# Softmax attention walked by token tile, with one norm chain for ten heads, and three operand sets prepared earlier, in an encoder block on one core

## The chip, the cores and the metric

The kernel runs on one core of one Trainium2 chip. The metric is the device time in microseconds (us) of one execution. Five engines work in parallel, each through its own list of instructions in order: PE (TensorE, matmuls; PEld is its weight load), DVE (VectorE), ACT (ScalarE), POOL (GpSimd, nearly unused here) and SP (SyncE, which issues all transfers between HBM and the on-chip memory).

## The reference

One layer over 1024 tokens of width 1024, all in float32. From `h = RMSNorm(x)` one projection gives the inputs of two branches. Cut to what matters here:

```python
h = _rms_norm(x, norm_mix_g[l]);  proj = h @ w_in[l]
# branch A: bidirectional gated linear attention, 4 heads, per-head RMSNorm, times silu(r)
y_gla = _gla_branch(g_q, g_k, g_v, g_r, g_lr_f, g_lr_b, ...) @ w_o_gla[l]
# branch B: softmax attention, 8 query heads on 2 key heads, head size 128, window +-128
q = _rope(_rms_norm(q, q_g), pos);  k = _rope(_rms_norm(k, k_g), pos)
p = exp(scores - m);  o = p / (p.sum() + exp(sink - m)) @ v
merged = sigmoid(gate_a) * y_gla + sigmoid(gate_b) * y_swa
x = x + merged @ w_out[l]
x = x + (silu(ff_gate) * ff_up) @ w_ffn_out[l]      # after a second RMSNorm
```

## The kernel before, in words

**Products.** Every float32 operand is split into a high part (an ACT copy to the float32r type) and a low part (a DVE subtraction), and every product is three matmuls: high x high, high x low, low x high (`mm3`, L77 to L80, and `product`, L811 to L817). A 512-column matmul is the unit of the work; 24 of them (8 pieces of the 1024 inner elements, three matmuls each) make one 128x512 result.

**The dense list.** Up to L912 the program interleaves two kinds of work on PE. One is `dense`, a list of generators (L552) whose steps are single 512-column matmuls: projections with tokens on the columns (`proj_f`, 48 steps each), projections with tokens on the rows (`proj_t`, 192 steps: 96 for the first half `s=0` of the tokens, 96 for the second) and `first_halves` (192 steps, the first half of the gate projections). In all 1824 steps. `fill(n)` issues n steps. The weights of a projection arrive 128x512 at a time by `next_unit`, two ahead. For `proj_t` the first pass splits each weight tile and stores both parts to HBM (`wkeep`, one load and two stores of 256 KB per 12 steps); the second pass loads both parts again (`wagain`, two loads, no splitting).

**Slots.** The other kind is the chain of small stages of the two attention branches, written into numbered slots. `slot(stages, n)` issues the slot's stages and spreads n dense steps between them, so that PE has matmuls to do while ACT and DVE prepare the next stage. The tables `GF` and `SF` give n. The order on PE is exactly the order of the program; on the other engines a scheduler sets the order from its own estimate when the kernel is built, and it can move an instruction far ahead of its place in the program.

**Gated linear attention** (slots with `GF`, 4 heads x 8 chunks). It opens with `fill(24)`, and its first PE stage, the gate matmuls of `g_gates` (`z`), needs `lrS`, the low-rank codes, which DVE writes last in `lr_out` (L313) after the norm statistics (`rsqrt`, L93 to L102). In slots 0 to 7 `x_sums` also forms differences of quarters of the normalised x (the sets T1, T2, 22, T3, T4) and stores them to HBM. They feed a seven-product scheme for the second half of the gate projections.

**Softmax attention** (slots with `SF`). There are 16 items: group g (4 heads) and token tile t. Before the change item n is `g, t = divmod(n, 8)`: all tiles of group 0, then all of group 1. An item goes through six consecutive slots: `a_prep` (load, squares, sums, norm factor, rotation), `a_turn` (transposes on PE), `a_scores`, `a_probs` (transposes of the probabilities), `a_out`. Keys are prepared by `k_prep` and `k_turn` for one tile per slot during the first 8 slots. The last four slots only drain the pipeline, with 15 dense steps each.

**The second half of the gates** (L900 to L912). `xpart` loads a set from HBM, ACT and DVE split it. The sets T1, T2 and 22 (12 tiles) are split here, each followed by 4 dense steps, then the remaining dense steps run, then `second_first(0)` forms a sum of weights `s1` (DVE, L808), splits it and multiplies it with T1 into bank Z; `second_rest(f)` follows for f = 0 to 7 with products by T2 (bank X), 22 (Z), T3 (X) and T4 (X). After each `second_rest(f)`, `prep_a(0, f)` prepares one of the eight tiles (`oa`) that the next stage, `branch_a(0)`, multiplies with w_oa: two loads, a sigmoid on ACT (L895), two DVE products, and the split (L825, L826).

**Staging.** `stage()` takes one of four 128x512 buffers for results that go out to HBM and for some loads.

## Time and profile before

| What | Value |
|---|---|
| Median of 3 runs (lowest, highest) | 1684.49 us (1682.74, 1684.93) |
| The profiled execution: its time, its span | 1679.58 us, 1677.3 us |
| PE busy, matmuls | 1655.2 us (99%), 7788 |
| DVE busy, ACT busy | 1237.9 us (74%), 857.1 us (51%) |
| Mean granted TensorE clock | 0.996 |
| Moved by the DMA engines | 300.13 MB, mean 179 GB/s |

The span runs from the first to the last instruction of the profiled execution. The clock is the share of full speed that TensorE was granted. Rows of the timeline begin with the start time and the duration in us; a bracket at the end of a row gives the idle time of that engine just before the instruction and what ended it. Matmuls overlap, so a row's duration is longer than the distance from start to start; the distance is what counts.

### The profile page before, as it was taken

How to read it: one execution, taken by the hardware profiler on the slowest of the kernel's cores; microseconds unless marked ns; L12 is line 12 of the kernel's file. 1: busy time of each engine (PE TensorE's matmuls, PEld its weight loads, DVE VectorE, ACT ScalarE, POOL GpSimd, SP SyncE). 2: the span in 40 equal slices, each digit the busy share in tenths (PEclk: the TensorE clock that was granted, in tenths of full speed). 3: DMA queues.
4: the chain of work that ended last, by engine and by line, in shares of the span. 5: the costliest groups of instructions: out<-in, count | busy, mean ns of one | idle time of the engine just before them, and what ended most of it. 6: DMA issues, size and time to landing. Idle time of an engine off the chain costs nothing.

```text
span 1677.3 us, 23798 instructions
## 1 busy us (share of the span) xinstructions
PE 1655.2 (99%) x7788; PEld 1372.9 (82%) x7788; DVE 1237.9 (74%) x2570; ACT 857.1 (51%) x1809; POOL 0.2 (0%) x4
## 2 busy tenths in 40 slices
PE   9999999999999998999999999999999999999999
PEld 6788888887888876887888888788888888888887
DVE  8786777853997767876673568887778877789755
ACT  7454677865687674334553556533333333344443
POOL 0000000000000000000000000000000000000000
PEclk9999999999999999999999999999999999999999
DMA  8875656668533238656764545344224543595433
GB/s 286 297 259 186 200 185 227 226 196 284 185 108 107 82 113 285 227 193 214 217 213 143 190 134 180 113 136 134 91 92 144 164 157 131 177 323 192 143 102 119
DMA packets 183547, 300.13 MB, mean 179 GB/s; under 512 B 20894, under 2 KB 46238, under 8 KB 183424
## 3 DMA queue, kind: packets, MB, share of 16 engines
q1 hardware_dynamic: 183424, 298.62, 54.4%
q8 instruction: 61, 1.00, 0.3%
q14 instruction: 62, 0.51, 0.1%
HBM read 203.12 MB, written 95.42 MB: 178 GB/s over the span
## 4 chain that ended last, share of the span: by engine, by line
PE 91%; DVE 3%; DMA 3%; ACT 2%; issue 1%; SPq 0%; ACTq 0%; DVEq 0%
PE mm L75 35%; PE ch L75 8%; PE mm L815 7%; PE mm L816 7%; PE mm L817 7%; PE mm L1177 7%; PE ch L1177 5%; PE ch L815 3%; PE ch L817 3%; PE ch L816 3%; PE mm L244 2%; PE ch L747 1%; DMA xr<-xT 1%; PE ch L546 0%; PE ch L697 0%
## 5 line engine op out<-in xcount | busy, mean ns | idle before, releaser
L69 ACT ACTIVATE wh<-wr 128x512 fp32r<-128x512 f32 x198 | 123.8, 628 | 115.1 <-PE mm L75 84.5
L71 DVE TENSOR_TENSOR wl<-wr,wh 128x512 fp32r<-128x512 f32 x198 | 135.7, 686 | 32.0 <-ACT wh L69 29.1
L794 ACT ACTIVATE wh<-ws 128x512 fp32r<-128x512 f32 x120 | 75.5, 631 | 148.7 <-PE mm L816 84.6
L75 PE MATMUL mm<-wl,xh 128*128 128x512 f32 x320 | 127.0, 397 | 1.2 <-DMA wl<-wl 1.2
L75 PE MATMUL mm<-wh,xh 128*128 128x512 f32 x320 | 127.7, 399 | 0.4 <-DVE st L136 0.4
L75 PE MATMUL mm<-wh,xl 128*128 128x512 f32 x320 | 127.9, 400 | 0.0
L75 PE MATMUL mm<-xh,wh 128*128 128x512 f32 x256 | 102.5, 401 | 0.3 <-ACT wh L69 0.3
L75 PE MATMUL mm<-xl,wh 128*128 128x512 f32 x256 | 102.0, 398 | 0.3 <-DVE xl L323 0.3
L794 ACT ACTIVATE wh<-wr 128x512 fp32r<-128x512 f32 x60 | 37.9, 632 | 105.4 <-issue 49.6
L795 DVE TENSOR_TENSOR wl<-ws,wh 128x512 fp32r<-128x512 f32 x120 | 82.1, 685 | 12.8 <-ACT wh L794 12.8
L75 PE MATMUL mm<-xh,wl 128*128 128x512 f32 x256 | 88.6, 399 | 0.0
L794 ACT ACTIVATE wh<-a 128x512 fp32r<-128x512 f32 x66 | 41.7, 632 | 90.6 <-PE mm L1177 42.4
L795 DVE TENSOR_TENSOR wl<-a,wh 128x512 fp32r<-128x512 f32 x66 | 45.5, 690 | 39.2 <-ACT wh L794 38.1
L75 PEld LDWEIGHTS mm<-wl,xh 128*128 128x128 f32 x320 | 60.5, 189 | 12.6 <-DMA wl<-wl 1.6
L75 PEld LDWEIGHTS mm<-wh,xh 128*128 128x128 f32 x320 | 60.7, 190 | 10.5 <-DVE st L136 0.8
L1177 PE MATMUL mm<-hh,wh 128*128 128x512 f32 x176 | 68.6, 390 | 0.5 <-DVE c L1115 0.5
L75 PEld LDWEIGHTS mm<-wh,xl 128*128 128x128 f32 x320 | 60.7, 190 | 10.2
L1177 PE MATMUL mm<-hl,wh 128*128 128x512 f32 x176 | 68.5, 389 | 0.0
L1177 PE MATMUL mm<-hh,wl 128*128 128x512 f32 x176 | 68.5, 389 | 0.0
L1150 DVE TENSOR_TENSOR hl<-hr,hh 128x512 fp32r<-128x512 f32 x77 | 52.7, 686 | 6.8 <-ACT hh L1149 6.7
L75 PEld LDWEIGHTS mm<-xl,wh 128*128 128x128 f32 x256 | 48.2, 188 | 7.6 <-DVE xl L323 0.6
L75 PEld LDWEIGHTS mm<-xh,wh 128*128 128x128 f32 x256 | 48.2, 188 | 7.4 <-ACT wh L69 0.5
(546 smaller groups left out, 4875.0 us busy)
## 6 DMA issues: line engine op xcount, KB each, us to landing
wr<-in_w_fi_dram SPq DMA_DIRECT2D x102, 256.0 KB, 2.8
wr<-in_w_f_dram SPq DMA_DIRECT2D x80, 256.0 KB, 3.4
wh<-wh SPq DMA_DIRECT2D x80, 256.0 KB, 2.9
wl<-wl SPq DMA_DIRECT2D x80, 256.0 KB, 3.0
B<-c SPq DMA_DIRECT2D x44, 256.0 KB, 2.1
T<-st SPq DMA_DIRECT2D x44, 256.0 KB, 2.6
a<-in_w_fo_dram SPq DMA_DIRECT2D x44, 256.0 KB, 5.3
hr<-T SPq DMA_DIRECT2D x44, 256.0 KB, 2.7
```

The costliest lines, as they stand in the source:

```text
L69: nc.scalar.activation(h, raw, AF.Copy)
L71: nc.vector.tensor_tensor(l, raw, h.bitcast(F32), op=ALU.subtract)
L75: nc.tensor.matmul(o, a, b, start=start, stop=stop)
L244: nc.tensor.matmul(Y[q], w[:, c], x, start=f0, stop=f1, skip_group_check=True)
L747: nc.tensor.transpose(pt[:, h], a.p[:, h, (kb - a.b0) * P:(kb - a.b0 + 1) * P], ident)
L794: nc.scalar.activation(h, src, AF.Copy)
L795: nc.vector.tensor_tensor(l, src, h.bitcast(F32), op=ALU.subtract)
L815: nc.tensor.matmul(o, h[:, c], x[kk][0], start=start and kk == 0, stop=False, skip_group_check=True)
L816: nc.tensor.matmul(o, h[:, c], x[kk][1], start=False, stop=False, skip_group_check=True)
L817: nc.tensor.matmul(o, l[:, c], x[kk][0], start=False, stop=kk == nk - 1, skip_group_check=True)
L1150: nc.vector.tensor_tensor(l, r, h.bitcast(F32), op=ALU.subtract)
L1177: nc.tensor.matmul(ys[m], a[:, c], b, start=f0, stop=f1, skip_group_check=True)
```

## The change

1. `rsqrt`: the correction step takes two DVE instructions ahead of the last one instead of three, and its first one now reads the result of the ACT exponential.
2. `proj_t` takes the half `s` as an argument. The second-half passes of `skv`, `sq0` and `sq1` move behind all three first-half passes; before, each was followed by its own second half.
3. The opening fill of the gated linear attention grows from 24 to 36 dense steps, and `x_sums` comes one slot later, behind the slot's stages.
4. Softmax attention goes by token tile: item n is `t, g = divmod(n, 2)`. One `prep(t)` per tile loads both groups of tile t and the keys and values of tile t+1, and computes one chain of squares, sums and norm factors for the ten heads; `a_rope` keeps the rotation. The output copy takes a buffer of `stage()` instead of one of its own.
5. The buffers `xn` live for the whole program, and `xpart` uses them. T1 and 22 are loaded and split in the four drain slots of the softmax attention (one tile of each per slot); only T2 stays behind them, with 8 dense steps after each tile.
6. `prep_a(0, f)` comes ahead of `second_rest(f)`, and `prep_a(0, 7)` ahead of `second_rest(6)`.

The number of matmuls and the number of issued transfers are the same.

```diff
@@ rsqrt
-            nc.vector.tensor_scalar(t, v, scale, epsv, op0=ALU.mult, op1=ALU.add)
-            nc.vector.tensor_tensor(t, t, l, op=ALU.mult)
-            nc.vector.scalar_tensor_tensor(t, t, -0.5, l, op0=ALU.mult, op1=ALU.mult)
+            nc.vector.scalar_tensor_tensor(t, l, -0.5 * scale, l, op0=ALU.mult, op1=ALU.mult)
+            nc.vector.scalar_tensor_tensor(t, v, epsv / scale, t, op0=ALU.add, op1=ALU.mult)
             nc.vector.scalar_tensor_tensor(dst, t, 1.5, l, op0=ALU.add, op1=ALU.mult)
...
         stg = root.enter_context(tc.tile_pool(name="stg", bufs=4))
+        xn = root.enter_context(tc.tile_pool(name="xn", bufs=4))
...
-        def proj_t(name, n):
-            for f in (wkeep, wagain):
-                plan.extend((lambda f=f, k=k: f(n, k)) for k in range(KT))
+        def proj_t(name, n, s):
+            plan.extend((lambda k=k: (wkeep, wagain)[s](n, k)) for k in range(KT))
...
-        dense += [proj_t("v0", 0), proj_f("q1", 2), proj_f("k1", 3), proj_f("q2", 4), proj_f("k2", 5),
-                  proj_t("v1", 1), proj_f("q3", 6), proj_f("k3", 7), proj_t("skv", 2), proj_t("sq0", 3),
-                  proj_t("sq1", 4)] + [proj_f(f"r{m}", 8 + m) for m in range(8)] + [first_halves()]
-
-        xn = glas.enter_context(tc.tile_pool(name="xn", bufs=4))
+        dense += [proj_t("v0", 0, 0), proj_t("v0", 0, 1), proj_f("q1", 2), proj_f("k1", 3), proj_f("q2", 4), proj_f("k2", 5),
+                  proj_t("v1", 1, 0), proj_t("v1", 1, 1), proj_f("q3", 6), proj_f("k3", 7), *(proj_t(nme, n, s) for s in range(2)
+                                                          for nme, n in (("skv", 2), ("sq0", 3), ("sq1", 4)))] + [proj_f(f"r{m}", 8 + m) for m in range(8)] + [first_halves()]
...
-            fill(24)
+            fill(36)
             for t in range(last + 1):
-                if t < 8:
-                    x_sums(t)
                 slot([(lambda v=at[t, j]: v[0](*v[1:])) if (t, j) in at else None for j in (0, 5, 4, 3, 2, 1)], share(GF, t))
+                if 1 <= t <= 8:
+                    x_sums(t - 1)
...
+        def prep(t):
+            sq = sw.tile([P, 10, P], F32, tag="sq", name=nm("sq"), bufs=1)
+            lo, hi = 8, 8
+            if t >= 0:
...
+                for g in range(2):
+                    need((f"sq{g}", t))
+                    nc.sync.dma_start(out=qr[:, 4 * g:4 * g + 4].rearrange("p a b -> p (a b)"), in_=scr[f"sq{g}", t])
+                nc.scalar.activation(sq[:, 0:8], qr, AF.Square)
+            if t + 1 < KT:
...
+                nc.scalar.activation(sq[:, 8:10], kv[:, 0:2], AF.Square)
+            ss = sw.tile([P, 10], F32, tag="ss", name=nm("ss"))
+            nc.vector.tensor_reduce(ss[:, lo:hi], sq[:, lo:hi], axis=mybir.AxisListType.X, op=ALU.add)
+            rs = sw.tile([P, 10], F32, tag="rs", name=nm("rs"), bufs=4)
+            rsqrt(rs[:, lo:hi], ss[:, lo:hi], 1.0, EPS * 128, eps128, sw, (P, hi - lo), f"sn{hi - lo}")
+            if t + 1 < KT:
+                keys[t + 1] = rope_k(kv, rs[:, 8:10], t + 1)
...
-            ob = sw.tile([P, 4, P], F32, tag="ob", name=nm("sob"))
+            ob = stage((P, 4, P))
...
         def xpart(q, k):
-            r = tp.tile([P, HT], F32, tag="xr", name=nm("xr"), bufs=8)
+            r = xn.tile([P, HT], F32, tag="xn", name=nm("xn"))
...
         for n in range(2 * KT):
-            g, t = divmod(n, KT)
+            t, g = divmod(n, 2)
...
-            todo[n + 1].append((a_prep, g, t))
-            if n < KT:
-                todo[n + 1].append((k_turn, n))
-                todo[n].append((k_prep, n))
-        order = (k_prep, a_prep, a_scores, a_turn, k_turn, a_out, a_probs)
+            todo[n + 1].append((a_rope, g, t))
+            if g == 0:
+                todo[n + 1].append((prep, t))
+                if t + 1 < KT:
+                    todo[n + 2].append((k_turn, t + 1))
+        order = (prep, a_rope, a_scores, a_turn, k_turn, a_out, a_probs)
...
                 slot([lambda e=e: e[0](*e[1:]) for e in v], share(SF, t))
+                if t >= 2 * KT + 2:
+                    assert len(dense) == 1
+                    for q in ("T1", "22"):
+                        xpart(q, t - 2 * KT - 2)
...
-            for q in ("T1", "T2", "22"):
-                for k in range(4):
-                    xpart(q, k)
-                    fill(4)
+            homes["T2"] = tp, "t2h{}", "t2l{}", 0
+            for k in range(4):
+                xpart("T2", k)
+                fill(8)
             fill(1 << 30)
...
             for f in range(len(PAIRS)):
+                if f < 7:
+                    prep_a(0, f)
+                if f == 6:
+                    prep_a(0, 7)
                 second_rest(f)
-                prep_a(0, f)
```

The order of instructions shows the change at three places. **First, DVE where the dense list ends.** `L808`/`L835` are the sums of weights (`ws`) for `second_first(0)` and `second_rest(0)`, `L795`/`L822` their low parts, `L247`/`L245` the results (`st`) of `first_halves`, of which PE's last dense matmul releases the last one; `L826`/`L774` are low parts of the operand sets. Before:

```order
L826 TENSOR_TENSOR xl_2126_8829<-xr_8826,xh_2125_8828 128x512
L808 TENSOR_TENSOR ws_8875<-wr_8871,wr_2132_8873 128x512
L808 TENSOR_TENSOR ws_8949<-ws_8875,wr_8869 128x512
L247 TENSOR_TENSOR st_8865<-mm_8756,rstd 128x512
L795 TENSOR_TENSOR wl_8879<-ws_8875,wh_8878 128x512
```

and, nine rows further on:

```order
L826 TENSOR_TENSOR xl_2157_8933<-xr_8930,xh_2156_8932 128x512
L826 TENSOR_TENSOR xl_2160_8939<-xr_8936,xh_2159_8938 128x512
L864 TENSOR_TENSOR nt_8946<-ch_8877,nt_8942 128x512
L869 TENSOR_TENSOR nt_8967<-mm_8948,nt_8942 128x512
L808 TENSOR_TENSOR ws_8969<-wr_2162_8944,ws_8949 128x512
```

Now:

```order
L245 TENSOR_TENSOR st_8512<-mm_8402,rstd 128x512
L71 TENSOR_TENSOR wl_8613<-wr_8609,wh_8611 128x512
L835 TENSOR_TENSOR ws_8675<-wr_8671,wr_2073_8673 128x512
L835 TENSOR_TENSOR ws_8761<-ws_8675,wr_8669 128x512
L245 TENSOR_TENSOR st_8575<-mm_8403,rstd 128x512
L822 TENSOR_TENSOR wl_8679<-ws_8675,wh_8678 128x512
L245 TENSOR_TENSOR st_8605<-mm_8579,rstd 128x512
L822 TENSOR_TENSOR wl_8764<-ws_8761,wh_8763 128x512
L774 TENSOR_TENSOR xl_2080_8697<-xn_8694,xh_2079_8696 128x512
L835 TENSOR_TENSOR ws_8781<-wr_2108_8756,ws_8761 128x512
L774 TENSOR_TENSOR xl_2083_8703<-xn_8700,xh_2082_8702 128x512
L245 TENSOR_TENSOR st_8633<-mm_8580,rstd 128x512
```

Before, the first sum `s1` (`ws_8875`) came just ahead of the last result of `first_halves`, behind the parts of 22, and the sum `s4` (`ws_8969`) came behind bank reads `nt` that wait for products. Now `s1`, `s2` and `s4` all stand ahead of the third result from the end (`st_8633`).

**Second, ACT around the last `oa` tile.** `sg` is the sigmoid of `prep_a`, `oah` the high part of its tile, `wh` of L69 the weights of `branch_a(0)`, `wh` of L794/L821 those of the second half of the gates. Before:

```order
L69 ACTIVATE wh_10040<-wr_10038 128x512
L69 ACTIVATE wh_10063<-wr_10061 128x512
L69 ACTIVATE wh_10081<-wr_10079 128x512
L895 ACTIVATE sg_9933<-st_9931 128x512
L825 ACTIVATE oah_2400_9937<-st_9929 128x512
```

Now:

```order
L903 ACTIVATE sg_9526<-st_9524 128x512
L821 ACTIVATE wh_9701<-ws_9699 128x512
L773 ACTIVATE oah_2296_9530<-st_9522 128x512
L821 ACTIVATE wh_9721<-wr_2316_9609 128x512
L69 ACTIVATE wh_9781<-wr_9779 128x512
```

The last `oah` stood behind the sixth weight tile of `branch_a(0)`; now it stands ahead of the first.

**Third, SP where the softmax attention begins.** `cosb` to `sink` are its constants, `kvr` the first keys and values, `sq_*` stores of a `proj_t` pass that is ending, `wh`/`wl` the kept weights of the pass that follows (the number after the name is the weight tile k). Before:

```order
L62 DMA cosb<-in_c_cos_dram 128x512
L62 DMA sinb<-in_c_sin_dram 128x512
L62 DMA band<-in_c_band_dram 128x384
L62 DMA qg<-in_qg_dram 128x128
L62 DMA kg<-in_kg_dram 128x128
L62 DMA sink<-in_sink_dram 128x8
L663 DMA kvr_5663<-skv_3683 128x512
L220 DMA sq_0_5704<-st_5705 128x512
L220 DMA sq_1_5714<-st_5715 128x512
L220 DMA sq_2_5724<-st_5725 128x512
L220 DMA sq_3_5734<-st_5735 128x512
L168 DMA wl_5744<-wl_2_5377 128x512
```

Now:

```order
L167 DMA wl_5741<-wl_3_4409 128x512
L62 DMA cosb<-in_c_cos_dram 128x512
L62 DMA sinb<-in_c_sin_dram 128x512
L62 DMA band<-in_c_band_dram 128x384
L62 DMA qg<-in_qg_dram 128x128
L62 DMA kg<-in_kg_dram 128x128
L62 DMA sink<-in_sink_dram 128x8
L661 DMA kvr_5669<-skv_3618 128x512
L218 DMA sq_6_5705<-st_5706 128x512
L218 DMA sq_7_5715<-st_5716 128x512
L167 DMA wh_5739<-wh_3_4407 128x512
```

Behind the constants the first weight part still to come was that of tile k=2, after four stores; now it is that of k=3, after two.

More of the change, by code (lines that the diff above doesn't have):

```diff
@@ L189, in proj_f @@
             return steps()
[L191 to L193 removed]
+        def proj_t(name, n, s):
+            plan.extend((lambda k=k: (wkeep, wagain)[s](n, k)) for k in range(KT))
             def steps():
[L196 removed]
+                if True:
                     b = [mmtile() for _ in range(4)]
@@ L625, in body, with rope_k @@
         nc.vector.tensor_tensor(qB[:, :, 64:128], sinb, gb_[0], op=ALU.mult)
[L627 to L645 removed]
+        nc.vector.tensor_scalar(kg, kg, 128 ** 0.5, None, op0=ALU.mult)
+        for h in range(8):
+            for s in range(2):
+                scr["b", h, s] = scratch(f"b{h}_{s}")
+        keys, att = {}, {}
+        def rope_k(raw, rs, t):
+            qn = sw.tile([P, 2, P], F32, tag="qn2", name=nm("qn"))
+            b = sw.tile([P, 2, P], F32, tag="sq2", name=nm("sq"))
+            for h in range(2):
+                nc.vector.scalar_tensor_tensor(qn[:, h], raw[:, h], rs[:, h:h + 1], kg, op0=ALU.mult, op1=ALU.mult)
+            c = cosb[:, t:t + 1].to_broadcast([P, 2, 64])
+            s = sinb[:, t:t + 1].to_broadcast([P, 2, 64])
             nc.vector.tensor_tensor(b[:, :, 0:64], qn[:, :, 64:128], s, op=ALU.mult)
@@ L764, in a_out, with xsplit, xpart @@
                                   in_=ob[:, h])
+        XT = {q: [] for q in ("T1", "T2", "22", "T3", "T4")}
+        def xsplit(pool, th, tl, src):
+            h = pool.tile([P, HT], FR, tag=th, name=nm(th))
+            l = pool.tile([P, HT], FR, tag=tl, name=nm(tl))
+            nc.scalar.activation(h, src, AF.Copy)
+            nc.vector.tensor_tensor(l, src, h.bitcast(F32), op=ALU.subtract)
+            return h, l
+        homes = {"T1": (xp, "xh{}1", "xl{}1", 0), "22": (xp, "xh{}1", "xl{}1", 4),
+                 "T3": (xp, "xh{}0", "xl{}0", 0), "T4": (xp, "xh{}0", "xl{}0", 4)}
+        def xpart(q, k):
+            r = xn.tile([P, HT], F32, tag="xn", name=nm("xn"))
+            nc.sync.dma_start(out=r, in_=scr[f"x{q}", k])
+            pool, th, tl, d = homes[q]
+            XT[q].append(xsplit(pool, th.format(k + d), tl.format(k + d), r))
         todo = [[] for _ in range(2 * KT + 6)]
+        todo[0].append((prep, -1))
+        todo[1].append((k_turn, 0))
         for n in range(2 * KT):
-            g, t = divmod(n, KT)
+            t, g = divmod(n, 2)
             todo[n + 5].append((a_out, g, t))
```

67 lines of the change are left out of this document (16 added, 51 removed).

## Prediction

> **What bounds the kernel now.** I read the page's first rows and its chain of waits first.
>
> ```profile
> span 1677.3 us, 23798 instructions
> PE 1655.2 (99%) x7788; PEld 1372.9 (82%) x7788; DVE 1237.9 (74%) x2570; ACT 857.1 (51%) x1809; POOL 0.2 (0%) x4
> PE 91%; DVE 3%; DMA 3%; ACT 2%; issue 1%; SPq 0%; ACTq 0%; DVEq 0%
> ```
>
> PE is the bound: 99% busy, 91% of the chain. The change leaves the number of matmuls as it is, so fewer DVE and ACT instructions are worth nothing in themselves; only stretches in which PE waits or runs slowly can be won or lost. The second view is therefore PE's own list of waits (engine and tile, what it waited for: us in total, times, longest).
>
> ```profile
> PE ch L815 <- ACT wh L794: 4.6, 2, 2.6
> PE mm L75 <- ACT oah L825: 3.2, 1, 3.2
> PE ch L75 <- DVE lrS L313: 1.9, 1, 1.9
> PE mm L75 <- DMA wl<-wl: 1.2, 1, 1.2
> PE ch L75 <- ACT ph L750: 1.2, 1, 1.2
> PE ch L817 <- DVE wl L795: 0.5, 1, 0.5
> PE mm L75 <- DVE st L136: 0.4, 1, 0.4
> ```
>
> Few waits are long, and each has a place that the change touches. What a wait costs is read from PE's timeline, since the matmuls after it may be slow too. First the undisturbed pace:
>
> ```profile
> 679.62 0.39 PE L815 MATMUL mm<-xh,wh 128*128 128x512 f32 x1
> 693.22 0.39 PE L815 MATMUL mm<-xh,wh 128*128 128x512 f32 x1
> ```
>
> Between these two rows stand 60 matmuls of 512 columns: 13.60 / 60 = 0.2267 us each. Now the end of the dense list, where the second half of the gates begins:
>
> ```profile
> 656.36 0.39 PE L244 MATMUL mm<-xh,wl 128*128 128x512 f32 x1
> ...
> 658.72 0.50 PE L815 MATMUL ch<-xh,wh 128*128 128x512 f32 x1 [1.98 <-ACT wh L794]
> ...
> 669.40 0.50 PE L815 MATMUL ch<-xh,wh 128*128 128x512 f32 x1 [2.58 <-ACT wh L794]
> ...
> 673.98 0.54 PE L815 MATMUL mm<-xh,wh 128*128 128x512 f32 x1
> ```
>
> From the first to the last row PE makes 37 steps (one dense, three products of 12). At the pace that is 37 x 0.2267 = 8.39 us; it took 17.62. So 9.23 us are lost, though the waits in it (1.98, 0.5, 2.58) are only 5.1 together. The rest is a slower clock, as one row of the table by stretches shows (us; busy us and count of PE, PEld, DVE, ACT, POOL; granted clock; DMA share; GB/s):
>
> ```profile
> 660.00:664.00 4.00, 4.00 (x11) 3.13 (x12) 3.20 (x6) 2.11 (x5) 0.00 (x0) 0.58 0.98 279
> ```
>
> PE waits for nothing here, yet 11 matmuls take 4 us at a granted clock of 0.58. So a wait of about 2 us is paid nearly twice. The Trainium skill, "TensorE: Matmul & The Clock Gate", section "What's actually happening", has the clock fall to half after an idle window of about 3.4 us; here it falls after an idle time of 1.98 us, so the measurement decides. By that rule the slow stretches would not come from these waits, none of which reaches 3.4 us; that is the third rival below.
>
> **The change part by part.**
>
> *The opening (parts 1 and 3).*
>
> ```profile
> 46.22 0.39 PE L75 MATMUL mm<-wh,xl 128*128 128x512 f32 x1
> 48.50 0.47 PE L75 MATMUL ch<-lrS,upS 98*128 98x256 f32 x2 [1.89 <-DVE lrS L313]
> ...
> 53.15 0.40 PE L75 MATMUL mm<-wh,xh 128*128 128x512 f32 x1
> ```
>
> PE issues its 24 dense steps and then waits for `lrS`. From 46.22 to 53.15 lie 13 dense steps and the pair of gate matmuls (0.31 us to the next start): 3.26 us at the pace, 6.93 as run, 3.67 lost. Twelve more steps are 12 x 0.2267 = 2.72 us, more than the wait of 1.89. Does `lrS` stay where it is?
>
> ```profile
> 39.12 0.68 DVE L102 SCALAR_TENSOR_TENSOR rstd<-rt,rl 128x512 f32<-128x512 f32 x1
> 47.14 1.21 DVE L313 TENSOR_TENSOR lrS<-lrf,lrS 32x1024 fp32r<-32x1024 f32 x1
> ```
>
> Each of the two 128x512 `rsqrt` chains loses one DVE instruction of about 0.69 us, and the weight split that stood inside the second chain moves behind it. Against that, the first instruction now needs ACT's exponential. I expect `rstd` up to 2 us sooner and `lrS` about 1 us sooner, since the low-rank matmuls and their ACT copies hold it from the other side. The wait for `st` (0.4, above) should go too. Worth 4.0; bounds 0 (`lrS` later by the 2.7) and 4.0. `x_sums` one slot later only takes DVE instructions away from here.
>
> *The order of the dense list (part 2).* The 1.2 us wait is at 414.33, for `wl` of weight tile k=2, whose load stood behind six constants and four result stores:
>
> ```profile
> 409.99 0.75 SPq L168 DMA_DIRECT2D wl<-wl  x1
> 405.00:430.00 25.00, 23.80 (x106) 19.32 (x106) 16.28 (x53) 10.64 (x27) 0.00 (x0) 1.00 0.96 327
> ```
>
> Now k=0 to 2 are loaded ahead of the constants and only k=3 follows, behind two stores: 12 steps, 2.72 us, more room than the 1.2 us that were short. Worth 1.2; bounds 0 and 1.2. The price: three splitting passes stand in a row, where every other pass had no splitting. Eight weight tiles of 0.69 us on DVE and 0.63 on ACT (the duration of a 128x512 subtraction and copy, in rows below), and 8 x 256 KB more traffic, come into a pass. The six passes of `skv`, `sq0` and `sq1` run from the first of these rows to the second, 576 steps, 30.5 us each.
>
> ```profile
> 247.52 0.48 PE L75 MATMUL mm<-wh,xh 128*128 128x512 f32 x1
> 430.83 0.39 PE L75 MATMUL mm<-xh,wh 128*128 128x512 f32 x1
> ...
> 280.00:305.00 25.00, 25.00 (x149) 21.50 (x148) 17.07 (x50) 16.77 (x47) 0.00 (x0) 1.00 0.68 208
> 305.00:330.00 25.00, 24.96 (x147) 21.52 (x146) 23.61 (x71) 23.25 (x69) 0.00 (x0) 1.00 0.73 247
> ```
>
> Of the two stretches the upper is mostly a reading pass, the lower a splitting one: DVE 23.61 of 25 and still only 0.04 us of PE idle. The upper gains 8 x 0.69 x 25 / 30.5 = 4.5 us and becomes like the lower. The cover is the distance between slots; if it is gone, late weights cost 1.2 us apiece, which is a rival below.
>
> *The softmax attention (part 4).* It removes 15 of 24 norm chains (squares, sums, logarithm, exponential, correction): together with part 1, DVE has 104 rows fewer in the instruction order, ACT 40.
>
> ```profile
> 455.00:480.00 25.00, 25.00 (x133) 21.28 (x133) 24.75 (x94) 20.88 (x56) 0.00 (x0) 1.00 0.32 101
> 580.00:605.00 25.00, 25.00 (x131) 20.78 (x130) 16.84 (x50) 16.66 (x41) 0.00 (x0) 1.00 0.34 106
> ```
>
> DVE was full while keys and queries were prepared together, and lighter later; by token tile the key work spreads over all 16 items. PE was at 25.00 of 25 in both, so this is worth 0 on PE. The new chain (load, ten squares, one sum, rotation of the next key) has a slot to run, as before. In the drain, the wait for `ph` (1.2) stays: its last items have four blocks of probabilities in place of five, so PE has less to cover them with, while ACT's order now puts the copies `ph` ahead of the last normalisation. Worth 0; bounds -2 to +2.
>
> *The sets T1 and 22 earlier (part 5).* Eight splits and eight loads move from the end of the dense list into the last attention slots; the scheduler spread them over the slots before the drain. There DVE has 16.84 and ACT 16.66 of 25 and the DMA share is 0.34 (row above): 8 x 0.69 and 8 x 0.63 fit. What held PE at 658.72 and 669.40:
>
> ```profile
> 657.26 0.69 DVE L808 TENSOR_TENSOR ws<-wr,wr 128x512 f32<-128x512 f32 x1
> ...
> 666.75 0.68 DVE L864 TENSOR_TENSOR nt<-ch,nt 128x512 f32<-128x512 f32 x1
> 667.35 0.68 DVE L869 TENSOR_TENSOR nt<-mm,nt 128x512 f32<-128x512 f32 x1
> 667.94 0.68 DVE L808 TENSOR_TENSOR ws<-wr,ws 128x512 f32<-128x512 f32 x1
> ...
> 658.04 0.63 ACT L794 ACTIVATE wh<-ws 128x512 fp32r<-128x512 f32 x1 [2.04 <-DVE ws L808]
> ```
>
> `s1` was formed at 657.26, after PE had finished the dense list, because DVE's queue held the low parts of 22, which waited for their loads. `s4` at 667.94 stood behind two bank reads, the second of which waits for the whole product by T2. In the new order `s1`, `s2` and `s4` stand ahead of the third-last result of the dense list, two products of 12 before its end, 5.4 us. The last load that `s1` needs stands on SP behind the ninth of the 16 results, seven products or 19 us ahead of the end. So both waits should go, with what followed: worth 9.2; bounds 0 and 9.2. What is late next: T3, wanted three products (8.2 us) after the end and splittable only once the dense list has read its old contents, two products before the end. That is 13.6 us for four splits of 0.69.
>
> *`prep_a` earlier (part 6).*
>
> ```profile
> 779.56 0.39 PE L75 MATMUL mm<-oah,wl 128*128 128x512 f32 x1
> 783.12 0.51 PE L75 MATMUL mm<-oah,wh 128*128 128x512 f32 x1 [3.17 <-ACT oah L825]
> ...
> 786.98 0.40 PE L75 MATMUL mm<-oah,wl 128*128 128x512 f32 x1
> ...
> 780.26 0.63 ACT L895 ACTIVATE sg<-st 128x512 f32<-128x512 f32 x1 [1.86 <-DMA st<-r]
> 782.44 0.63 ACT L825 ACTIVATE oah<-st 128x512 fp32r<-128x512 f32 x1 [1.55 <-DVE st L897]
> ```
>
> Nine steps from 779.56 to 786.98 took 7.42 us in place of 2.04: 5.38 lost to the eighth `oa` tile. It now stands ahead of the first w_oa weights on ACT; the program has it two rounds of five products (27 us) sooner. Two `prep_a` in a row take all four staging buffers, and the results of that round wait for them; PE goes on, because bank Z and X of the next round are other buffers. Worth 5.4; bounds 0 and 5.4.
>
> **Sum**: 4.0 + 1.2 + 9.2 + 5.4 = 19.8 us at most. I take off 1.8, half of what the opening's wait costs with its slow stretch (3.67), for a place in the rearranged slots that the trace of before can't show: 18.0. The profiled execution would go from 1679.58 to 1661.6; it lies 4.9 under the median shown, so the median goes from 1684.49 to **1666.5**.
>
> **Rivals.**
>
> *The waits move into the attention slots.* ACT and DVE work in order, and the eight splits wait for loads and for PE to finish with the old contents. If two slots end with such a wait, at 3.67 each, the gain is 19.8 - 7.3 = 12.5: 1672.0. For it: DVE at 24.75 of 25 early on. Against: the splits come where DVE has 8 us to spare in 25.
>
> *The first sums stay late.* Part 5 then doesn't do what it says: DVE's order is right, but the w_f loads come late behind stores on SP. Gain 19.8 - 9.2 = 10.6: 1673.9. Against: the last of them is issued 19 us ahead.
>
> *The slow stretches are not due to the waits.* Then only the waits go, 11.8 us by the list: 1684.5 - 11.8 = 1672.7. The Trainium skill's page on the clock gate would have it so, by its 3.4 us. Against: the waits of 1.89, 1.98, 2.58 and 3.17 us are each part of a stretch that lost far more than the wait.
>
> *Slower: three splitting passes starve PE of weights.* The 24 tiles need loads, stores, ACT and DVE at once; at the 1.2 us of the wait at 414.33 each, all late, that is 28.8 us: 1684.5 - 19.8 + 28.8 = 1693.5. It eats the gain from 17 of 24 tiles late and makes the kernel slower by a measurable amount from 20. Against: a single such pass (23.61 of 25 on DVE, DMA 0.73) cost PE 0.04 us.
>
> **How the numbers follow.** Forecast 0.80, the first three rivals 0.07, 0.05 and 0.02, the slower one 0.06. The likeliest gives 1666.5. Its own range runs from 1661 (all 19.8, 2 more in the drain, 1.8 for the spread of the runs downwards) to 1670; the rivals on the same side reach 1673.9, and with the runs' spread and a term missed beside it I go to 1678. A measurement of this kernel can tell 0.2% (3.4 us) from no change. Faster by more than that: 0.90, the first four cases less a little for several misses at once; within it: 0.05; slower: 0.05, most of the last rival.
>
> **What would show it.** In the profile after: no wait of PE at the products of line 842 and none for `oah`, `lrS` or `wl`; granted clock 1.00 in all stretches behind the first 50 us; about 1659 us of span with the same count of matmuls. Wrong would be: waits for `ph`, `sqh` or `kTh` of over 1 us in the attention slots, or for `wl` between 250 and 350 us.

## The result and the profile after

The changed kernel takes 1670.46 us (median; 1668.81 to 1673.36), beside 1684.71 of the kernel before on the same chip: a ratio of 0.9919, with a 95% interval of 0.9907 to 0.9931. So it is faster by 14.2 us (11.6 to 15.7); forecast were 18.0 and a time of 1666.5. A later repeat, on another chip, gave 1668.66 us and 0.9909 (0.9889 to 0.9929). The profiled execution took 1668.81 us.

The page's first rows and its chain of waits, of the changed kernel:

```profile
span 1666.7 us, 23629 instructions
PE 1650.6 (99%) x7788; PEld 1370.6 (82%) x7788; DVE 1229.2 (74%) x2466; ACT 850.9 (51%) x1771; POOL 0.2 (0%) x4
PE 88%; DVE 5%; DMA 3%; ACT 3%; issue 1%; SPq 0%; DVEq 0%; ACTq 0%
```

The matmuls are the same 7788, DVE has 104 instructions fewer. The span is 10.6 us shorter, not the 18 that the prediction's "about 1659" asked for. That is also less than the 14.2 of the medians: the profiled execution of the kernel before lies 5.1 us under its median, that of the changed one 1.7. PE's list of waits (what it waited for: us in total, times, longest) says where to look:

```profile
PE ch L75 <- ACT sqh L703: 2.5, 1, 2.5
PE mm L842 <- DVE u L1111: 2.0, 1, 2.0
PE ch L75 <- DVE sh L473: 1.7, 2, 0.9
PE mm L75 <- DMA wh<-wh: 1.2, 1, 1.2
...
PE mm L842 <- DVE st L851: 0.8, 1, 0.8
PE mm L1188 <- DVE c L1126: 0.7, 1, 0.7
```

The waits for `oah`, `lrS` and the first sums' `wh` are gone; a new one, for `sqh`, heads the list. PE's timeline shows the first gate matmuls (`lrS`) and the change from the dense list (line 242) to the second half of the gates (line 842) without a gap, then the places where a wait is left:

```profile
48.28 0.40 PE L75 MATMUL ch<-lrS,upS 98*128 98x256 f32 x2
...
413.76 0.50 PE L75 MATMUL mm<-wh,xh 128*128 128x512 f32 x1 [1.17 <-DMA wh<-wh]
...
444.32 0.60 PE L700 MATMUL ch<-ident,qn 128*128 128x128 f32 x4
...
445.91 0.40 PE L75 MATMUL mm<-xh,wh 128*128 128x512 f32 x1
448.84 0.58 PE L75 MATMUL ch<-kTh,sqh 128*128 128x256 f32 x1 [2.53 <-ACT sqh L703]
...
657.13 0.39 PE L242 MATMUL mm<-xh,wl 128*128 128x512 f32 x1
657.35 0.39 PE L842 MATMUL ch<-xh,wh 128*128 128x512 f32 x1
...
1060.53 0.47 PE L842 MATMUL mm<-bt30h,wh 128*128 128x512 f32 x1 [2.04 <-DVE u L1111]
```

The table by stretches (us; busy us and count of PE, PEld, DVE, ACT, POOL; granted clock; DMA share; GB/s) has the clock at these places:

```profile
448.00:452.00 4.00, 3.16 (x10) 2.65 (x11) 1.47 (x5) 3.88 (x9) 0.00 (x0) 0.53 0.28 106
452.00:456.00 4.00, 4.00 (x16) 3.33 (x15) 3.01 (x7) 0.60 (x3) 0.00 (x0) 0.61 0.23 66
660.00:664.00 4.00, 3.91 (x18) 2.96 (x17) 3.25 (x6) 3.20 (x6) 0.00 (x0) 1.00 0.97 337
```

Between 660 and 664, where the kernel before ran at 0.58, it is now 1.00; the half clock stands behind the wait for `sqh` instead.

For the whole account I added up, from PE's timeline, what each gap between two starts exceeds its pace (0.2267 us per 512 columns; for the other shapes the median of the kernel before, used for all four executions), in us by stretch of the program:

| stretch (times of about) | before | changed | changed, repeat | 32 steps (below) |
|---|---|---|---|---|
| opening, 40 to 60 | 4.5 | 0.1 | 0.1 | 0.1 |
| GLA slots, 90 to 160 | 4.3 | 5.6 | 5.4 | 5.4 |
| end of the GLA, 395 to 430 | 1.7 | 1.7 | 1.6 | 0.7 |
| first attention slots, 435 to 465 | 0.8 | 6.4 | 3.9 | 1.1 |
| middle slots, 465 to 595 | 5.4 | 5.9 | 5.5 | 4.5 |
| drain, 595 to 645 | 4.4 | 2.1 | 1.8 | 2.8 |
| second half of the gates, 645 to 720 | 9.4 | 1.7 | 1.6 | 2.1 |
| start of branch a, 750 to 795 | 5.6 | 0.2 | 0.4 | 0.2 |
| start of the FFN, 1030 to 1085 | 1.4 | 2.7 | 2.0 | 1.5 |
| all, with what lies between | 54.0 | 43.4 | 39.4 | 36.1 |
| span | 1677.3 | 1666.7 | 1662.7 | 1659.3 |

The differences of the sums (10.6, 14.6, 17.9 against before) are those of the spans (10.6, 14.6, 18.0), so the table holds all of it. The three terms that the prediction set highest are won: 4.4, 7.7 and 5.4. What is missing is mostly the 5.6 us in the first attention slots.

What stands on ACT there in the kernel before, and then in the changed kernel (with the last input of the exponentials, on DVE):

```profile
445.46 0.58 ACT L700 ACTIVATE sqh<-ch 128x512 fp32r<-128x512 f32 x1
...
446.20 0.20 ACT L727 ACTIVATE es<-es 128x4 f32<-128x4 f32 x1
```

```profile
445.46 0.42 ACT L662 ACTIVATE sq<-kvr 128x256 f32<-128x256 f32 x1 [5.05 <-DMA kvr<-skv]
445.54 0.16 DVE L729 TENSOR_TENSOR es<-sink,mx 128x4 f32<-128x4 f32 x1
445.78 0.19 ACT L730 ACTIVATE es<-es 128x4 f32<-128x4 f32 x1
...
447.63 0.58 ACT L733 ACTIVATE p<-p,nm,rs 128x256 f32<-128x256 f32 x1
...
448.21 0.57 ACT L703 ACTIVATE sqh<-ch 128x512 fp32r<-128x512 f32 x1
```

PE makes the query transposes of the second item at 444.32; ACT could copy them to `sqh` at 445, but in its queue stand the squares of a key tile, which waited 5.05 us for their load, and then `es` and four exponentials of the first item. Two theories follow. **A**: the load is late, because `kvr` has a single buffer. **B**: the order on ACT is wrong for the moment, the exponentials standing ahead of `sqh`, while their inputs come late from DVE.

### The profile page after: what moved, and what is told of

It reads as the page before. It is cut to its first block, busy times and chain, and to the rows that moved or that the text cites. A ratio compares the mean times of both kernels' runs of the same rounds, so it can differ in the third digit from the quotient of the medians.

```text
span 1666.7 us, 23629 instructions
## 1 busy us (share of the span) xinstructions
PE 1650.6 (99%) x7788; PEld 1370.6 (82%) x7788; DVE 1229.2 (74%) x2466; ACT 850.9 (51%) x1771; POOL 0.2 (0%) x4
## 4 chain that ended last, share of the span: by engine, by line
PE 88%; DVE 5%; DMA 3%; ACT 3%; issue 1%; SPq 0%; DVEq 0%; ACTq 0%
PE mm L75 35%; PE ch L75 8%; PE mm L1188 7%; PE mm L842 6%; PE mm L843 6%; PE mm L844 6%; PE ch L1188 5%; PE ch L843 3%; PE ch L842 3%; PE ch L844 3%; PE mm L242 2%; PE ch L750 1%; DMA xn<-xT 1%; DMA xn<-in_xT_dram 0%; DVE ws L835 0%
## 5 line engine op out<-in xcount | busy, mean ns | idle before, releaser
L69 ACT ACTIVATE wh<-wr 128x512 fp32r<-128x512 f32 x198 | 123.7, 628 | 108.8 <-PE mm L75 84.9
L821 ACT ACTIVATE wh<-ws 128x512 fp32r<-128x512 f32 x120 | 75.4, 630 | 136.6 <-PE mm L843 74.8
L822 DVE TENSOR_TENSOR wl<-ws,wh 128x512 fp32r<-128x512 f32 x120 | 82.2, 685 | 12.3 <-ACT wh L821 12.3
L821 ACT ACTIVATE wh<-wr 128x512 fp32r<-128x512 f32 x60 | 37.9, 631 | 103.5 <-issue 47.9
L821 ACT ACTIVATE wh<-a 128x512 fp32r<-128x512 f32 x66 | 41.7, 631 | 91.5 <-PE ch L1188 42.3
L822 DVE TENSOR_TENSOR wl<-a,wh 128x512 fp32r<-128x512 f32 x66 | 45.5, 690 | 40.1 <-ACT wh L821 38.6
```

What stands on the lines that cost most here:

```text
L69: nc.scalar.activation(h, raw, AF.Copy)
L821: nc.scalar.activation(h, src, AF.Copy)
L822: nc.vector.tensor_tensor(l, src, h.bitcast(F32), op=ALU.subtract)
```

## The experiments

All edits are to the changed kernel. Times are medians; the ratio is to the kernel before on the same chip (its medians there were 1683.1 to 1683.7).

**Two buffers for the raw keys** (A against B):

```
-  kv = sw.tile([P, 4, P], F32, tag="kvr", name=nm("kvr"), bufs=1)
+  kv = sw.tile([P, 4, P], F32, tag="kvr", name=nm("kvr"))
```

> Two buffers for the raw key tile kvr in place of one; nothing else. In the profile of the changed kernel PE waits 2.53 us for sqh at 448.84 (line 703), and the stretch 440 to 460 loses 6.3 us against PE's pace. Theory A (the load of the keys is the cause: ACT's square of kvr stands ahead of the copy sqh and waits 5.05 us for a load that can only start when DVE has read the single buffer): the wait goes, the stretch loses 0.5 as in the kernel before, about 1664.7 us, 5.8 less than the changed kernel. Theory B (the order on ACT is the cause: the four exponentials of the first item stand ahead of sqh, and their input es came from DVE only at 445.70, 0.24 us after the square began): sqh stays behind the exponentials, the wait stays at 2 us or more, 1670 us.

1669.9 us, 0.9917 (0.9904 to 0.9931): nothing gained. Rows of ACT, DVE and PE:

```profile
440.55 0.40 ACT L662 ACTIVATE sq<-kvr 128x256 f32<-128x256 f32 x1
...
446.71 0.16 DVE L729 TENSOR_TENSOR es<-sink,mx 128x4 f32<-128x4 f32 x1
446.81 0.42 ACT L670 ACTIVATE vSh<-kvr 128x256 fp32r<-128x256 f32 x1 [5.24 <-DMA kvr<-skv]
447.14 0.19 ACT L730 ACTIVATE es<-es 128x4 f32<-128x4 f32 x1
...
449.57 0.57 ACT L703 ACTIVATE sqh<-ch 128x512 fp32r<-128x512 f32 x1
...
450.19 0.39 PE L75 MATMUL ch<-kTh,sqh 128*128 128x256 f32 x1 [2.51 <-ACT sqh L703]
```

The square now waits for nothing, 6.6 us ahead of `es`, and PE still waits 2.51 us. But the wait for a load has not left ACT's queue: the copy of the values `vSh` (the other half of a `kvr` tile), just ahead of `es`, now waits 5.24 us for it. So the edit does not remove what A names, and the unchanged time alone does not refute A. DVE's row does: the input of `es` was ready at 446.87, hardly after ACT's wait for the load ended at 446.81, and in the changed kernel at 445.70, 0.24 after the square began there. Without the wait the exponentials, and `sqh` behind them, could have come about 0.3 us sooner, not 2.5. So A falls by this row: the 5.05 us on ACT's row were the longest wait in view and not the cause.

**Transposes ahead of the scores:**

```
-  order = (prep, a_rope, a_scores, a_turn, k_turn, a_out, a_probs)
+  order = (prep, a_rope, a_turn, a_scores, k_turn, a_out, a_probs)
```

> Within an attention slot the query transposes of the next item stand ahead of the scores of the present one, so that ACT's copy sqh stands ahead of the exponentials; the single buffer kvr stays. Theory B (the order on ACT is the cause): the 2.53 us wait for sqh goes and the stretch 440 to 460 loses under 1 us, about 1664.7 us, 5.8 less than the changed kernel. Theory A (the late load of the keys is the cause): ACT still waits about 5 us at the square of kvr; if sqh now stands ahead of the square too, the time is the same as by B, and the first experiment tells them apart; if it stands behind, the wait stays and the time is 1670 us. A third way: the scores start a block of dense steps later, the exponentials and the transposes of the probabilities come late, and PE waits for ph instead by 1 to 3 us: 1668 to 1673 us.

1665.95 us, 0.9904 (0.9886 to 0.9922). The first attention slots lose 1.5 us in place of 6.4, as B wants. The time is 4.5 us less than the changed kernel's by the medians and 2.5 by the ratios, whose intervals overlap. Smaller waits come up in later slots, among them one for `pl` (like the third way of the expectation, at the lower end of its 1 to 3 us), and in this execution the wait near 414 was longer:

```profile
417.62 0.50 PE L75 MATMUL mm<-wh,xh 128*128 128x512 f32 x1 [2.48 <-DMA wh<-wh]
...
538.88 0.41 PE L75 MATMUL ch<-kTh,sqh 128*128 128x384 f32 x1 [1.01 <-DVE pl L754]
```

**`prep_a` late again** (part 6 undone):

```
   for f in range(len(PAIRS)):
-      if f < 7:
-          prep_a(0, f)
-      if f == 6:
-          prep_a(0, 7)
       second_rest(f)
+      prep_a(0, f)
```

> Part 6 alone is undone: each prep_a stands again behind its round of the second half of the gates. The prediction's term: PE waits about 3.2 us for oah at the start of branch a and loses 5.4 us with the slow stretch behind it: 1675.9 us. If the early prep_a cost something where it stands now (the round's results wait for staging buffers), undoing it gives that back and the time rises by less than 4 us: below 1674.5 us.

1674.07 us, 0.9952 (0.9936 to 0.9967): 3.6 us more by the medians, 5.6 by the ratios: between the two expectations. The wait is back and branch a's start loses 6.8 us:

```profile
774.95 0.50 PE L75 MATMUL mm<-oah,wh 128*128 128x512 f32 x1 [4.28 <-ACT oah L773]
```

**T1 and 22 behind the attention again** (part 5 undone, with the four buffers `xn`):

```
   # behind each slot from the 19th on:
-  for q in ("T1", "22"):
-      xpart(q, t - 2 * KT - 2)
   # in the dense list behind the attention:
-  for k in range(4):
-      xpart("T2", k)
-      fill(8)
+  for q in ("T1", "T2", "22"):
+      for k in range(4):
+          xpart(q, k)
+          fill(4)
```

> Part 5 alone is undone: the sets T1 and 22 are loaded and split in the dense list behind the attention, 4 steps between two tiles as in the kernel before (through the four buffers xn). The prediction's term: PE waits again at the first products of the second half of the gates (line 842, or the line it has here) and loses 9.2 us there: 1679.7 us. Rival (the splits in the attention's last slots cost PE time there, where 600 to 640 and 685 lose about 2 us in the changed kernel): 1677 to 1678 us. If the first sums were late for another reason, their place in the queues, the time would be unchanged, 1670.5 us.

1670.5 us, 0.9925 (0.9911 to 0.9938): no measurable loss, which the prediction's 9.2 did not allow. At its place 5.6 us were lost, between the 1.7 of the changed kernel and the 9.4 of the kernel before; the start of the FFN, on the other hand, lost 1.2 in place of 2.7. The next run shows why only half of the term came back.

**The same with the eight buffers `xr`:**

```
-  r = xn.tile([P, HT], F32, tag="xn", name=nm("xn"))
+  r = tp.tile([P, HT], F32, tag="xr", name=nm("xr"), bufs=8)
```

> Part 5 undone once more, now with the eight load buffers of the kernel before (tag xr) in place of the four shared ones (xn). In the fourth experiment, with four, s1 was formed at 647.6, 8 us ahead of the end of the dense list, and PE lost 5.3 us there (waits of 1.89 and 0.93 for s4's split), in place of 9.1 in the kernel before and 1.2 in the changed one. If the number of buffers, and with it the order of DVE's queue, is what made s1 late in the kernel before, PE now waits for wh at the first product of the second half of the gates and loses about 9 us: 1670.5 + 7.9 = 1678.4 us. If it is the attention's end that made s1 late there (the drain of the kernel before), the loss stays near 5: 1671 to 1674.5 us.

1681.17 us, 0.9982 (0.9970 to 0.9993): 12.5 us more than the changed kernel measured beside it, and 2.8 more than expected. The second half of the gates loses 14.2 us. PE's list of waits:

```profile
PE ch L838 <- ACT wh L817: 8.1, 2, 4.2
```

The loads of w_f on SP's queue, and `s1` on DVE:

```profile
655.45 0.93 SPq L826 DMA_DIRECT2D wr<-in_w_f_dram  x2
...
660.83 0.69 DVE L831 TENSOR_TENSOR ws<-wr,wr 128x512 f32<-128x512 f32 x1 [2.50 <-DMA wr<-in_w_f_dram]
```

`s1` waits for its own w_f load, not for low parts of 22 ahead of it on DVE, as the prediction reads it in the kernel before. On SP's queue the loads of the twelve parts go one after the other as long as buffers are free; nine of them stand between 644.18 and the two w_f loads at 655.45. With four buffers in the run above, w_f's loads come ahead of the last parts, and the first sum was formed 13 us earlier:

```profile
647.59 0.69 DVE L831 TENSOR_TENSOR ws<-wr,wr 128x512 f32<-128x512 f32 x1
```

So fewer load buffers alone take away a good half of this loss (14.2 to 5.6 us) and the earlier sets the rest (to 1.7). The earlier sets with eight buffers were not tried.

**Attention by group again** (part 4 undone; the separate norm chains for keys and queries return, and with them the order of items):

```
-  t, g = divmod(n, 2)
+  g, t = divmod(n, KT)
...
-  order = (prep, a_rope, a_scores, a_turn, k_turn, a_out, a_probs)
+  order = (k_prep, a_prep, a_scores, a_turn, k_turn, a_out, a_probs)
```

> Part 4 alone is undone: softmax attention by group, with a chain of norms for the keys of a tile and one for the queries of a group, as in the kernel before; the other parts stay. Theory B (the new order of the attention puts the exponentials of the first item ahead of sqh while DVE is late): the wait for sqh is gone and the stretch 440 to 460 loses 0.5 again, 5.8 us less; the drain loses 3 us again (the wait of 1.2 for ph at the end, with what follows): about 1667.7 us. Rival (the wait comes from the dense list's new order or the earlier sums, not from part 4): the wait stays, the drain loses its 3 us: 1673.5 us. The prediction's own term for part 4 was 0: 1670.5 us.

1665.92 us, 0.9893 (0.9877 to 0.9909). ACT's queue has `sqh` ahead of the exponentials here:

```profile
447.82 0.60 ACT L697 ACTIVATE sqh<-ch 128x512 fp32r<-128x512 f32 x1 [0.79 <-PE ch L694]
...
449.20 0.19 ACT L724 ACTIVATE es<-es 128x4 f32<-128x4 f32 x1
```

The first slots lose 0.9 us (6.4 in the changed kernel), the middle ones 5.7 (5.9), the drain 3.3 (2.1). Beside these other parts, part 4 costs 4.5 us in the attention slots by this account, and 2.7 to 4.5 by the medians (against the repeat and the first measurement).

**The dense list in its old order** (part 2 undone):

```
-  proj_t("v0", 0, 0), proj_t("v0", 0, 1), ...
-  *(proj_t(nme, n, s) for s in range(2) for nme, n in (("skv", 2), ("sq0", 3), ("sq1", 4)))
+  proj_t("v0", 0), ...
+  proj_t("skv", 2), proj_t("sq0", 3), proj_t("sq1", 4)
```

> Part 2 alone is undone: the two halves of each row-tile projection stand together again, so the three splitting passes no longer stand in a row, and k=2 of the last projection is loaded behind the six constants. The prediction's term: 1.2 us more, 1671.7 us. By the profile of the changed kernel, in which PE still waits 1.17 us at 413.76 (now for k=3): no difference, 1670.5 us. The slower rival of the prediction (splitting passes in a row starve PE): the time falls, and the small losses between 240 and 345 with it; they are 3 us in all, so at most to 1668 us.

1672.05 us, 0.9930 (0.9916 to 0.9944): 1.6 us more by the medians, near the predicted 1.2 and within the uncertainty. PE's two waits there:

```profile
291.76 0.38 PE L75 MATMUL ch<-thb,q2b 128*128 128x256 f32 x1 [1.17 <-ACT kb L495]
...
412.85 0.50 PE L75 MATMUL mm<-wl,xh 128*128 128x512 f32 x1 [1.89 <-DMA wl<-wl]
```

The stretch 395 to 430 loses 2.5 us in place of 1.7; the wait for `kb` is one that the changed kernel does not have. Three splitting passes in a row starve nothing: without them the time does not fall.

**24 dense steps ahead of the GLA** (part 3 undone in its main point):

```
-  fill(36)
+  fill(24)
```

> Only the number of dense steps ahead of the GLA's first slot goes back from 36 to 24. The prediction's term: PE waits about 1.9 us for lrS and loses 3.7 us: 1674.2 us. Rival (the shorter correction chain of part 1 brings lrS so much sooner that 24 steps would do): PE waits under 0.9 us and loses under 1.5 us: below 1672 us.

1667.81 us, 0.9904 (0.9887 to 0.9921): not slower. The time lies in the range of the rival expectation (below 1672), but for another reason: PE does wait for `lrS`, longer than the 0.9 us that the rival allows. Whether it is faster than the changed kernel stays open, as the intervals overlap. DVE's row for `lrS`, PE's wait for it, and ACT's order in the first attention slots:

```profile
45.84 1.22 DVE L311 TENSOR_TENSOR lrS<-lrf,lrS 32x1024 fp32r<-32x1024 f32 x1
...
47.20 0.48 PE L75 MATMUL ch<-lrS,upS 98*128 98x256 f32 x2 [1.26 <-DVE lrS L311]
...
442.69 0.58 ACT L703 ACTIVATE sqh<-ch 128x512 fp32r<-128x512 f32 x1
...
444.31 0.60 ACT L733 ACTIVATE p<-p,nm,rs 128x256 f32<-128x256 f32 x1 [1.04 <-DVE nm L727]
```

The opening loses 1.7 us (4.5 before, 0.1 with 36 steps): parts 1 and 3 without the 12 steps have already won 2.8, and the steps are worth 1.6. And the wait for `sqh` is gone, because here the copy stands ahead of the exponentials. The 12 steps are not extra work: they come off the end of the same list, and every projection shifts 12 steps against the attention's slots. With that, DVE's and ACT's instructions of the projections fall differently between those of the attention, and the scheduler writes another order.

**32 dense steps.** In the instruction order, counts of 24 to 34 put `sqh` ahead of `es`, 36 to 44 put it behind.

```
-  fill(36)
+  fill(32)
```

> Only the number of dense steps ahead of the GLA's first slot changes, from 36 to 32. By theory B, now in this form: the 12 steps taken ahead shift the whole dense list against the slots, and with 36 the scheduler puts ACT's exponentials of the first item ahead of the copy sqh of the second; with 32 sqh stands ahead of them in the instruction order, as with 24. So the 2.53 us wait for sqh goes, with its slow stretch (5.8 us), and 8 steps more than 24 (1.8 us) still cover the 1.26 us that PE waited for lrS with 24: about 1664.7 us. Rival (the wait of the changed kernel comes from DVE's total load in the first attention slots, whatever the order on ACT): PE still waits over 1.5 us for sqh, 1668 to 1670.5 us.

1662.33 us, 0.9874 (0.9853 to 0.9894): 6.3 us less than the changed kernel measured beside it (five runs of 1661.14 to 1664.85, six of 1664.79 to 1671.58), the fastest of all. ACT's rows and PE's list of waits:

```profile
444.14 0.60 ACT L703 ACTIVATE sqh<-ch 128x512 fp32r<-128x512 f32 x1 [0.23 <-PE ch L700]
...
445.62 0.60 ACT L733 ACTIVATE p<-p,nm,rs 128x256 f32<-128x256 f32 x1 [0.88 <-DVE nm L727]
```

```profile
PE mm L842 <- DVE st L851: 1.9, 1, 1.9
PE mm L75 <- DVE ones L86: 1.0, 1, 1.0
PE mm L842 <- DVE u L1111: 0.8, 1, 0.8
```

No wait for `sqh` or `lrS` is in the list. B is borne out by a change of one number in another part of the program. Over all runs it is the same: each by-tile kernel with 36 steps and the attention's order unchanged has the wait for `sqh` (2.4 to 3.6 us), the others do not.

**The changed kernel again**, measured beside the run with 32 steps:

> The changed kernel itself, beside the others of this call: 1670.5 us, waits of 2.5 us for sqh near 449 and about 2 us for u near 1060. The wait for wh near 414 was between 0 and 2.5 us in executions of the same program up to there; if it varies by execution it may take any value in that range.

1668.66 us, 0.9909. The waits are where they were (2.36 for `sqh`, 1.29 for `u`, 1.01 near 414). The clock behind the first is not:

```profile
448.00:452.00 4.00, 3.36 (x18) 2.81 (x19) 2.76 (x9) 3.85 (x8) 0.00 (x0) 1.00 0.16 61
452.00:456.00 4.00, 4.00 (x26) 3.37 (x25) 4.00 (x14) 1.69 (x5) 0.00 (x0) 1.00 0.27 70
```

**Transposes first, `x_sums` late, constants early:**

```
-  order = (prep, a_rope, a_scores, a_turn, k_turn, a_out, a_probs)
+  order = (prep, a_rope, a_turn, a_scores, k_turn, a_out, a_probs)
...
-  if 1 <= t <= 8:
-      x_sums(t - 1)
+  if t == 16:
+      cosb, sinb, band = ...   # the three load_const calls, moved here into pool xp
+  if 30 <= t <= 37:
+      x_sums(t - 30)
```

> Three edits beside the changed kernel, in places that its profile names: the query transposes ahead of the scores (as in the second experiment, 4.5 us less than the changed kernel there), the eight calls of x_sums in slots 30 to 37 of the GLA in place of 1 to 8 (DVE is busy 20.7 of 25 us between 100 and 125, where PE loses 3.8 us to waits for sh and sl, and about 8.8 of 25 between 350 and 400), and the three large constants of the attention loaded in slot 16 instead of at its start, ahead of the weights for which PE waits 1.2 to 2.5 us near 414. If each place loses nothing afterwards: 1670.5 - 4.5 - 3.8 - 1.3 = about 1661 us. Rival: the moved sums and their stores delay the loads at the end of the GLA, so that PE waits there for weights; the gain of the second edit comes back as a loss and the time is 1664 to 1667 us.

1670.13 us, 0.9925 (0.9908 to 0.9943): neither expectation, no gain over the changed kernel. The end of the GLA lost 0.4 us, so the constants were worth their 1.3 and the moved sums did not delay loads there (the scheduler put the constants' loads as far ahead as 19.93 us). But the GLA slots 90 to 160 lost 8.9 us instead of 5.6, with a wait on ACT that the changed kernel does not have,

```profile
103.32 0.39 PE L75 MATMUL ch<-vh,kth 128*128 128x256 f32 x1 [2.22 <-ACT kth L462]
```

and the middle slots 8.6 instead of 5.9. Taking DVE's work away at 100 to 125 did not remove the waits there. That the moved sums caused the new loss is not shown: the run with transposes first alone lost 8.0 in the GLA slots, the next one 9.8, both with the sums where they were.

**34 steps and the constants early:**

```
-  fill(36)
+  fill(34)
...
+  if t == 16:
+      cosb, sinb, band = ...   # as above
```

> The changed kernel with 34 dense steps in place of 36 (sqh ahead of the exponentials in ACT's order) and the three large constants of the attention loaded in slot 16 of the GLA, not at the attention's start ahead of weight tiles. If both the wait for sqh (5.8 us) and the one near 414 (1.3 us) go: 1670.5 - 7.1 = 1663.4 us. If the wait near 414 comes from the stores of results and not from the constants: 1664.7 us, the same as with 32 steps alone.

1666.62 us, 0.9888 (0.9867 to 0.9910): above both expectations. The wait near 414 is gone (0.4 us in the stretch), the one for `sqh` too, but PE waits at the same place for the low part:

```profile
451.12 0.56 PE L75 MATMUL ch<-kTh,sql 128*128 128x256 f32 x1 [2.19 <-DVE sql L705]
```

The first attention slots lost 5.0 us, and the GLA slots 9.8. On DVE `sql` stood behind the score chain, as `sqh` had stood on ACT. B has to be put more widely: both halves of the split must stand ahead of the first item's softmax, on ACT and on DVE, and the instruction order of ACT alone does not tell it.

## Why the prediction came out as it did

- *Direction and size.* Faster by 14.2 us where 18.0 were forecast. The measured time lies nearer to the first rival (1672.0) than to the forecast, and one slot did get the wait which that rival expects in two; its cause, though, was not the eight splits, and with 32 steps the wait is absent with the splits in place. Part of the nearness to 18.0 is luck: the drain won 2.3 us that the sum had at 0.
- *Opening (4.0).* 4.4 won. DVE begins the last step of `lrS` at 45.84 with 24 steps, 1.3 us sooner than before, as the "about 1 us" said.
- *Order of the dense list (1.2).* 0.0 to 0.1 at its place in the two executions compared; a wait for the next tile, k=3, took over, behind the same constants. "More room than the 1.2 us that were short" failed. That wait ran from none (24 steps) to 2.48 us (transposes first), and it was absent in both runs that loaded the constants early. In one of these that may be the shift of the list, since with 24 and 32 steps it is absent with the constants where they were. Undoing the part cost 1.6, within the noise of it.
- *Softmax attention (0, bounds -2 to +2).* This is the step that failed: in sum about -3.8 in the first profile (drain +2.3, middle -0.5, first slots -5.6), outside the bounds, and about -0.5 in the second, where the clock did not fall. The prediction's own sign of being wrong, a wait for `sqh` of over 1 us, came in both. "The new chain has a slot to run, as before" looked at the lengths of the work and not at its order on ACT and DVE. "ACT's order now puts the copies `ph` ahead" was read for the drain, where it went better than said (the wait for `ph`, which was to stay, is gone); the same reading of `sqh` and `es` in the first slots would have shown that the copy stands behind the exponentials.
- *T1 and 22 (9.2).* 7.7 won; 12.5 when it is undone with eight buffers. The mechanism is in the main that of the prediction: `s1` and `s4` late on DVE behind loads, though with eight buffers the late load was that of w_f. What it didn't have is that the number of load buffers is a cause of its own.
- *`prep_a` (5.4).* 5.4 won.
- *The allowance (1.8).* It was the right kind of term, "a place in the rearranged slots", and mis-sized: 5.6 in the first profile and 3.0 in the second, according to whether the clock falls behind the wait.
- *`fill(36)`.* The prediction costed the 12 steps only where they are spent. What the last four of them cost where they are taken away, through the shift of the list against the slots, was 6.3 us (36 against 32 steps), more than the 1.6 that all twelve are worth at the opening.
- *Slow stretches not due to the waits.* Where a wait went (opening, gates, branch a), the slow stretch went with it, and the new wait brought a new one in one of two executions. That rival falls.
- *Three splitting passes.* Falls, by the run with the old list.
- *Left open.* The wait for `u` at the start of the FFN (0.5 to 2.0 us over the runs) and the 1.1 to 1.3 us more in the GLA slots were not traced to a part of the change; the GLA slots lose 5.0 to 9.8 us from run to run, also where the edit lies far behind them.

## What to carry to other kernels

When a scheduler writes the order, moving a few steps of filler is an edit to every place behind them: read the new instruction order, on all engines, where the filler now meets the tightest hand-over, and try two or three neighbouring counts. When PE waits for a copy, ask what stands ahead of that copy in its queue and which input of those came last; the longest wait printed on the queue may end hardly later than another input was ready, and then it is worth almost nothing. Before a reordering gets the credit for a wait, check whether a buffer count alone would remove it.

## What was not expected of the hardware

The same program lost 6.4 us in the first attention slots with a wait of 2.53 and 3.9 us with a wait of 2.36 in its two profiles. In the first the nine matmuls of 256 columns and nine of 512 from 448.84 to 455.06 took 6.22 us, twice the 3.1 of the pace, at granted clocks of 0.53 and 0.61; in the second the clock stayed at 1.00. The kernel before had its clock down to 0.58 after a wait of 1.98. So a wait of 2 to 2.5 us sometimes costs about its own length and sometimes twice that. The spread of 7 us between runs of one kernel goes along with the clock: in the repeat the fastest run (1664.79) had a mean granted clock of 1.000, the slowest (1671.58) 0.997, and 0.003 of the span of 1666.7 us is about 5 us, an estimate from these figures. That the clock of these runs fell behind this one wait is not shown. The Trainium skill, "TensorE: Matmul & The Clock Gate", section "What's actually happening", says that the gate's window of about 3.4 us runs freely, not tied to the kernel's start. That fits two outcomes for one wait, but by its rule of a whole idle window none of these waits would be long enough, and here the measurement decides.
